# A hybrid attention and recurrence layer on one core: the same program, ordered by the scheduler's timeline mode

## The chip, the core and the metric

The kernel runs on one core of a Trainium2 chip. Its engines are TensorE (PE, with PEld for its weight loads), VectorE (DVE), ScalarE (ACT), GpSimd (POOL) and SyncE (SP), which issues all DMA transfers of this kernel from one queue. The metric is the device time of one execution in microseconds (us), as the median of several runs. A profile is one execution recorded by the hardware profiler; its times count from the first instruction.

## The reference

One layer over 16 learned meta tokens and 1024 frames of width 1024, all in float32, cut to what matters:

```python
u = rms_norm(h, norm_mix_w)
fq, fk, fv, ff, hq, hf, hi, hg = split(u @ w_in)
# A: forgetting attention, 8 heads x 64, causal; c = cumsum(log_sigmoid(ff + bias))
fox = softmax(fq @ fk.T / 8 + c_i - c_j, causal) @ fv
# B: gated recurrence, 4 heads with a 128 x 128 state
S_t = diag(f_t) S_{t-1} + k_t v_t^T;  o_t = S_t^T q_t
hgrn = rms_norm(o, hgrn_norm_w) * silu(hg)
h = h + concat(fox, hgrn) @ w_out
u = rms_norm(h, norm_ffn_w)
h = h + (silu(u @ w_gate) * (u @ w_up)) @ w_down      # inner width 2816
out = rms_norm(h, norm_final_w)[:, 16:]
```

## The kernel before

Every large matrix product is done in float32r in three passes: each operand is split into a high part (`hi`, a cast on ScalarE, L135) and the rest (`lo`, a subtraction on VectorE, L136), and `mm3` (L167 to L169) multiplies hi by hi, hi by lo and lo by hi into the same PSUM bank. So each tile that TensorE multiplies needs first a load, then ScalarE, then VectorE.

The program is written with a tile framework. The kernel's Python code records instructions stage by stage; the framework then gives each engine its own list, in an order that a scheduler chooses when the context is left, assigns the buffers of the pools, and adds the semaphore waits that the data and the buffers need. On the chip an engine works through its list strictly in that order: an instruction that waits holds up all that stand behind it on its engine, and a transfer that SP has not issued holds up all transfers behind it. The scheduler may move an instruction of a later stage ahead of an earlier one when it finds it ready. A few places are pinned by hand (`after`, `hold`, `keep_in_program_order`).

The stages, in the order in which the code records them:

- **Norm and first projection** (L219 to L256): RMSNorm of nine row tiles, transposes on TensorE, `hi` columns projected.
- **Recurrence** (`hgrn_proj` L349, `hgrn_compute` L398) of four heads, with `fox_v` (L310, the value projection of the attention, evacuated at L323 and L324) between them. A head's recurrence is a chain of small steps in two units of 512 frames: exponentials on ScalarE, adds on VectorE, small products on TensorE.
- **Attention** (`fox_compute` L627), four pairs of heads. `fox_proj` (L512) projects keys and queries of the next pair (bank `dense`, evacuated at L522/L523 and L530/L531). `fox_group` (L552) treats 256 queries of one head: scores on TensorE (L569, L570, bank `g`), added to the bias with a running minimum on VectorE (L575), exponential on ScalarE (L580), transposes back on TensorE (L588, L600, bank `tr`), split on ScalarE and VectorE (L604, L605; L590, L591), product with the values on TensorE (L610, bank `o`), sums on VectorE (L622, L639). The projection of a pair is independent of the attention of the pair before it, so it is work that TensorE can do while the attention waits for VectorE.
- **Output projection and second norm** (`out_proj` L735, `norm2` L761, `pair` L793), and the sums of the first blocks of the FFN.
- **FFN, gate and up** (L970, 22 blocks): products of half blocks by a scheme with seven instead of eight products; the weights' sums are made on VectorE (`ffn_sums`, L836 to L839), the results go to DRAM (`h_store`).
- **FFN, down** (L1149 on): 7 products of 6 pieces each. For each piece `stage` loads a part of the intermediate result (`h_st`, L992) and a part of `w_ffn_down`, splits both, and `mults` (L1024) multiplies: 24 matmuls for a full piece, 12 for the last of a product. The weight quarters B11, B12, B21, B22 are loaded ahead into buffers of their own (`fetch`, L984), six pieces each, and VectorE makes the combinations T1 to T4 of them (L1048, L1052, L1056, L1060), which later products use. A table (`work`, L1132) says at which piece the code records each load and combination: B12 at pieces 10 to 15, T1 at 15 to 20, and so on.
- **End**: the four row tiles of the last product are finished one after the other by hand (L1165 on), each with its sum, its norm (`final_half`, `final`) and its store.

## Time and profile before

| what | value |
|---|---|
| median of three runs | 1305.54 us (1304.8 to 1307.61) |
| the profiled execution, device time | 1305.52 us |
| its span, first to last instruction | 1303.8 us |
| busy: PE, DVE, ACT, POOL | 1270.7 (97%), 909.3 (70%), 621.2 (48%), 125.9 (10%) us |
| moved by DMA | 146.38 MB, 112 GB/s over the span |
| mean granted TensorE clock | 0.995 |

The profiled execution's 1305.52 us are its span and 1.7 us around it, and lie 0.02 us under the median. TensorE is busy nearly all of the span, so its list, and where that list has to wait, sets the time. The views used further on: the busy time of each engine in a stretch, groups of equal instructions with the mean time of one, and what ended the idle time before an instruction.

### The profile page before, as it was taken

What the parts mean: (1) busy time and instruction counts of PE and PEld (TensorE: products, weight loads), DVE (VectorE), ACT (ScalarE), POOL (GpSimd) and SP (SyncE); (2) the same over time, 40 slices, a digit from 0 to 9 for tenths busy, and PEclk for the clock granted to TensorE, in tenths of its full rate; (3) what the DMA queues carried; (4) which work ended last, traced back from release to release, by engine and by line L of the source; (5) the groups of instructions that cost most, each with busy time, mean ns of one, the idle gap of its engine ahead of it and who ended that gap; (6) DMA issues with size and microseconds to landing.
All of it is one profiled execution on the core that took longest, in us unless ns stands there. A gap on an engine that the chain in (4) does not pass through costs nothing.

```text
span 1303.8 us, 18528 instructions
## 1 busy us (share of the span) xinstructions
PE 1270.7 (97%) x6553; PEld 1065.4 (82%) x6553; DVE 909.3 (70%) x1889; ACT 621.2 (48%) x1334; POOL 125.9 (10%) x257
## 2 busy tenths in 40 slices
PE   7999999999999999899999999999999999999997
PEld 6888898988888888688868888888888888888886
DVE  6448657574687877796798766666666654697777
ACT  6347656464666665664453333233323323433364
POOL 1131101010334342210000000000000000000000
PEclk8999999999999999999999999999999999999999
DMA  7232212123321211633314323333332336954442
GB/s 253 73 98 58 74 44 73 58 58 118 92 79 45 69 52 47 187 100 119 125 49 138 125 83 115 121 111 103 118 121 74 113 121 248 317 188 151 121 169 82
DMA packets 135197, 146.38 MB, mean 112 GB/s; under 512 B 6984, under 2 KB 95368, under 8 KB 135104
## 3 DMA queue, kind: packets, MB, share of 16 engines
q1 hardware_dynamic: 135104, 145.19, 34.6%
q8 instruction: 52, 0.85, 0.3%
q14 instruction: 41, 0.34, 0.1%
HBM read 105.98 MB, written 39.19 MB: 111 GB/s over the span
## 4 chain that ended last, share of the span: by engine, by line
PE 80%; DVE 8%; ACT 5%; DMA 3%; issue 2%; POOL 2%; SPq 0%; POOLq 0%; DVEq 0%; ACTq 0%
PE pb L167 10%; PE pb L169 10%; PE pb L168 10%; PE dense L169 8%; PE dense L167 8%; PE dense L168 8%; PE g L169 4%; PE g L167 4%; PE g L168 4%; PE o L610 2%; PE tr L600 2%; PE g L569 1%; PE g L570 1%; PE g L446 1%; DMA w_st<-in_w_in_dram 1%
## 5 line engine op out<-in xcount | busy, mean ns | idle before, releaser
L167 PE MATMUL dense<-u_hi,w_hi 128*128 128x512 f32 (+2 forms) x384 | 141.7, 369 | 0.0
L169 PE MATMUL dense<-u_hi,w_lo 128*128 128x512 f32 (+2 forms) x384 | 141.3, 368 | 0.0
L168 PE MATMUL dense<-u_lo,w_hi 128*128 128x512 f32 (+2 forms) x384 | 140.9, 367 | 0.0
L168 PE MATMUL pb<-T_lo,bh 128*128 128x512 f32 x352 | 137.2, 390 | 0.2
L169 PE MATMUL pb<-T_hi,bl 128*128 128x512 f32 x352 | 137.1, 390 | 0.1
L167 PE MATMUL pb<-T_hi,bh 128*128 128x512 f32 x352 | 136.9, 390 | 0.2 <-ACT bh L135 0.2
L135 ACT CAST bh<-sS 128x512 fp32r<-128x512 f32 x88 | 54.3, 621 | 144.3 <-PE pb L168 70.3
L135 ACT CAST h_hi<-h_st 128x1024 fp32r<-128x1024 f32 (+1 forms) x43 | 41.8, 971 | 83.7 <-PE o L168 38.2
L168 PEld LDWEIGHTS pb<-T_lo,bh 128*128 128x128 f32 x352 | 66.1, 188 | 15.0 <-DVE T_lo L136 1.1
L169 PEld LDWEIGHTS dense<-u_hi,w_lo 128*128 128x128 f32 x384 | 72.9, 190 | 6.2
L167 PEld LDWEIGHTS pb<-T_hi,bh 128*128 128x128 f32 x352 | 66.1, 188 | 14.6 <-ACT bh L135 0.6
L167 PEld LDWEIGHTS dense<-u_hi,w_hi 128*128 128x128 f32 x384 | 72.6, 189 | 6.5
L168 PEld LDWEIGHTS dense<-u_lo,w_hi 128*128 128x128 f32 x384 | 72.6, 189 | 6.4
L169 PEld LDWEIGHTS pb<-T_hi,bl 128*128 128x128 f32 x352 | 66.1, 188 | 14.2 <-DVE bl L136 0.4
L167 PE MATMUL pb<-w_hi,h_hi 128*128 128x512 f32 x198 | 77.3, 391 | 0.0
L169 PE MATMUL pb<-w_hi,h_lo 128*128 128x512 f32 x198 | 77.2, 390 | 0.0
L168 PE MATMUL pb<-w_lo,h_hi 128*128 128x512 f32 x198 | 77.2, 390 | 0.0
L136 DVE TENSOR_TENSOR w_lo<-w_st,w_hi 128x1024 fp32r<-128x1024 f32 (+1 forms) x41 | 49.6, 1210 | 35.4 <-ACT w_hi L135 35.4
L136 DVE TENSOR_TENSOR h_lo<-h_st,h_hi 128x1024 fp32r<-128x1024 f32 (+1 forms) x43 | 48.3, 1124 | 30.2 <-ACT h_hi L135 29.9
L167 PE MATMUL g<-B_hi,w_hi 128*128 128x512 f32 x168 | 66.6, 396 | 0.9 <-ACT p L865 0.9
L169 PE MATMUL g<-B_hi,w_lo 128*128 128x512 f32 x168 | 66.5, 396 | 0.0
L168 PE MATMUL g<-B_lo,w_hi 128*128 128x512 f32 x168 | 66.3, 395 | 0.0
(861 smaller groups left out, 3328.5 us busy)
## 6 DMA issues: line engine op xcount, KB each, us to landing
w_st<-in_w_in_dram SPq DMA_DIRECT2D x24, 512.0 KB, 4.2
w_st<-in_w_ffn_gate_dram SPq DMA_DIRECT2D x22, 512.0 KB, 3.8
w_st<-in_w_ffn_up_dram SPq DMA_DIRECT2D x22, 512.0 KB, 3.9
B<-in_w_ffn_down_dram SPq DMA_DIRECT2D x20, 512.0 KB, 6.3
h_st<-S SPq DMA_DIRECT2D x20, 512.0 KB, 3.8
h_st<-A SPq DMA_DIRECT2D x15, 512.0 KB, 4.4
A<-g SPq DMA_DIRECT2D x22, 256.0 KB, 2.0
S<-u SPq DMA_DIRECT2D x22, 256.0 KB, 3.0
```

The costliest lines, as they stand in the source:

```text
L135: later(act.copy(hi, src))
L136: return later((engine or vec).tensor_sub(lo, src, f32(hi)))
L167: pe.matmul(o, lhsT=ah, rhs=bh, start=first, stop=False, skip_group_check=skip)
L168: pe.matmul(o, lhsT=ah, rhs=bl, start=False, stop=False, skip_group_check=skip)
L169: pe.matmul(o, lhsT=al, rhs=bh, start=False, stop=last, skip_group_check=skip)
L446: m = pe.matmul(gb[:, k * P:(k + 1) * P], lhsT=X[:, k * P:(k + 1) * P], rhs=X[:, 256 + k * P:256 + (k + 1) * P], start=True, stop=True)
L569: pe.matmul(sc[:, :w], lhsT=QA[:, P * i:P * (i + 1)], rhs=KS[:, c0:c0 + w], start=True, stop=False)
L570: pe.matmul(sc[:, :w], lhsT=QB[:, P * ii:P * (ii + 1)], rhs=KS[:, c0:c0 + w], start=False, stop=True)
L600: pe.transpose(pt[:, o + ii * P:o + (ii + 1) * P], Ss[ii][:, c:c + P], ident)
L610: m = pe.matmul(ob[:, q0:256], lhsT=vt[:, blk, :], rhs=r[:, q0:256], start=blk == NT, stop=blk == 2 * g + 1 and i == 3)
```

## The change

The context that records and orders the program is opened with another option. Nothing else is edited.

```diff
-    with _tile.TileContext(nc) as tc:
+    with _tile.TileContext(nc, schedule_with_timeline_sim=True) as tc:
         hybrid_trunk(tc, *args)
```

With the option the scheduler decides what is ready by a timeline of engines and transfers instead of a list of simple durations. The instructions are the same, 6329 matmuls, 1197 on ScalarE, 389 transfers and so on, with the same operands; their order on every engine differs, and with it which buffer each gets and when it comes free. The first 70 us and the gate-and-up stage keep nearly the same order. In the other stages the lists differ as these three places show.

**TensorE, attention of the third pair of heads.** `g_56..` and `g_57..` are score banks of that pair, `o_5626` its value product, `KS0_5233` its keys, and `dense_6103` the projection of the fourth pair. Before:

```order
L569 MATMUL g_5696<-KS0_5233,QA0_5235 128x392
L570 MATMUL g_5696<-KS0_5233,QB_5670 128x392
L167 MATMUL dense_6103<-u_hi_134,w_hi_6070 128x512
L610 MATMUL o_5626<-mz0_3670,v1_5316 128x256
L569 MATMUL g_5700<-KS0_5233,QA0_5235 128x392
L570 MATMUL g_5700<-KS0_5233,QB_5670 128x392
L168 MATMUL dense_6103<-u_lo_135,w_hi_6070 128x512
L610 MATMUL o_5626<-PH_5637,v1_5316 128x256
```

With the change the same scores and transposes stand without a projection between them:

```order
L569 MATMUL g_5700<-KS0_5233,QA0_5235 128x392
L570 MATMUL g_5700<-KS0_5233,QB_5670 128x392
L569 MATMUL g_5765<-KS1_5234,QA1_5236 128x328
L570 MATMUL g_5765<-KS1_5234,QB_5755 128x328
L600 MATMUL tr_5642<-ident_118,S__5601 128x128
L600 MATMUL tr_5642<-ident_118,S__5613 128x128 x2
L610 MATMUL o_5626<-mz0_3670,v1_5316 128x256
L569 MATMUL g_5769<-KS1_5234,QA1_5236 128x328
L570 MATMUL g_5769<-KS1_5234,QB_5755 128x328
```

The projection `dense_6103` now stands one pair earlier, in one run behind the transposes of the second pair (`S__4307`, `tr_4369`):

```order
L600 MATMUL tr_4369<-ident_118,S__4307 128x128
L600 MATMUL tr_4369<-ident_118,S__4323 128x128
L169 MATMUL dense_6074<-u_hi_134,w_lo_6065 128x348
L167 MATMUL dense_6103<-u_hi_134,w_hi_6070 128x512
L168 MATMUL dense_6103<-u_lo_135,w_hi_6070 128x512
L169 MATMUL dense_6103<-u_hi_134,w_lo_6071 128x512
```

So the projections, which were spread between the steps of the attention, are drawn together and earlier.

**VectorE, second product of the down stage.** `h_lo` and `w_lo` are the rests of the pieces that TensorE multiplies next; `T_k` and `B_k` (the tile's own number ends the name) are the combinations for later products. Before:

```order
L136 TENSOR_TENSOR h_lo<-h_st,h_hi 128x1024
L136 TENSOR_TENSOR w_lo<-B_3_11283,w_hi 128x1024
L1072 TENSOR_TENSOR r_11313<-r_11313,g 128x512
L136 TENSOR_TENSOR h_lo<-h_st,h_hi 128x1024 x2
L136 TENSOR_TENSOR w_lo<-B_4_11309,w_hi 128x1024
L136 TENSOR_TENSOR h_lo<-h_st,h_hi 128x512
L136 TENSOR_TENSOR w_lo<-B_5_11349,w_hi 128x512
L1048 TENSOR_TENSOR T_0_11646<-B_0_11467,B_0_11387 128x1024
```

With the change, from the same `w_lo` on:

```order
L136 TENSOR_TENSOR w_lo<-B_3_11283,w_hi 128x1024
L1060 TENSOR_TENSOR B_0_11165<-B_0_11387,B_0_11165 128x1024
L1048 TENSOR_TENSOR T_1_11685<-B_1_11505,B_1_11427 128x1024
L1048 TENSOR_TENSOR T_2_11721<-B_2_11531,B_2_11089 128x1024
L1052 TENSOR_TENSOR B_1_11427<-B_1_11429,T_1_11685 128x1024
L1056 TENSOR_TENSOR B_1_11505<-B_1_11429,B_1_11505 128x1024
L1052 TENSOR_TENSOR B_2_11089<-B_2_11469,T_2_11721 128x1024
L1056 TENSOR_TENSOR B_2_11531<-B_2_11469,B_2_11531 128x1024
L1048 TENSOR_TENSOR T_3_11746<-B_3_11570,B_3_11127 128x1024
L1060 TENSOR_TENSOR B_1_11205<-B_1_11427,B_1_11205 128x1024
L136 TENSOR_TENSOR h_lo<-h_st,h_hi 128x1024
```

Nine combinations now stand between that `w_lo` and the next `h_lo`, and five more (four of full size, one half) between it and the `h_lo` after it.

**SP, the same place.** `h_st<-A_0_68`, `A_1_69`, `A_2_70` are the loads of the first three pieces of the second product. Before:

```order
L992 DMA h_st<-A_0_68 128x2x512
L984 DMA B_2_11245<-in_w_ffn_down_dram 128x2x512
L1067 DMA r_11247<-h_dram 128x1024
L992 DMA h_st<-A_1_69 128x2x512
L984 DMA B_3_11283<-in_w_ffn_down_dram 128x2x512
L1067 DMA r_11285<-h_dram 128x1024
L992 DMA h_st<-A_2_70 128x2x512
```

With the change twelve weight loads stand between the first two of them, the last eleven of which are:

```order
L984 DMA B_0_11387<-in_w_ffn_down_dram 128x2x512
L984 DMA B_0_11389<-in_w_ffn_down_dram 128x2x512
L984 DMA B_1_11427<-in_w_ffn_down_dram 128x2x512
L984 DMA B_1_11429<-in_w_ffn_down_dram 128x2x512
L984 DMA B_0_11467<-in_w_ffn_down_dram 128x2x512
L984 DMA B_2_11469<-in_w_ffn_down_dram 128x2x512
L984 DMA B_1_11505<-in_w_ffn_down_dram 128x2x512
L984 DMA B_3_11507<-in_w_ffn_down_dram 128x2x512
L984 DMA B_2_11531<-in_w_ffn_down_dram 128x2x512
L984 DMA B_4_11533<-in_w_ffn_down_dram 128x2x512
L984 DMA B_3_11570<-in_w_ffn_down_dram 128x2x512
L992 DMA h_st<-A_1_69 128x2x512
```

The weights of four products are now asked for at the start of the second one.

## The prediction

> **What bounds the kernel now.** First the page's first lines, then the chain of waits that ended last.

> ```profile
> span 1303.8 us, 18528 instructions
> PE 1270.7 (97%) x6553; PEld 1065.4 (82%) x6553; DVE 909.3 (70%) x1889; ACT 621.2 (48%) x1334; POOL 125.9 (10%) x257
> PE 80%; DVE 8%; ACT 5%; DMA 3%; issue 2%; POOL 2%; SPq 0%; POOLq 0%; DVEq 0%; ACTq 0%
> ```

> TensorE is busy for 1270.7 of 1303.8 us. It idles 33.1 us, and that is all that an order can win; what it can lose is read from VectorE, the next busiest. Its 909.3 us would fit beside TensorE's work with room to spare, but only if they are spread well, so the second view is the windows by stage: microseconds, then each engine's busy time, the granted clock, the DMA share and GB/s.

> ```profile
> 0.00:100.00 100.00, 93.26 (x457) 77.49 (x458) 54.77 (x114) 48.20 (x98) 22.75 (x45) 0.97 0.45 143
> 100.00:357.00 257.00, 251.08 (x1604) 223.60 (x1603) 166.48 (x399) 152.98 (x469) 27.71 (x44) 1.00 0.23 69
> 357.00:592.00 235.00, 225.37 (x1413) 191.83 (x1413) 187.74 (x607) 149.89 (x335) 75.40 (x169) 1.00 0.28 85
> 592.00:700.00 108.00, 105.23 (x478) 83.65 (x477) 86.32 (x173) 51.44 (x113) 0.00 (x0) 1.00 0.31 99
> 700.00:1092.00 392.00, 391.82 (x1713) 321.09 (x1712) 260.02 (x385) 123.38 (x184) 0.00 (x0) 1.00 0.35 112
> 1092.00:1296.00 204.00, 203.94 (x896) 167.73 (x894) 150.40 (x202) 93.38 (x134) 0.00 (x0) 1.00 0.56 187
> 1296.00:1303.80 7.80, 0.00 (x0) 0.00 (x0) 3.59 (x14) 1.89 (x6) 0.00 (x0) 0.65 0.48 185
> ```

> Behind each window stand its length and TensorE's busy time. Their difference is TensorE's idle time: 6.7 us in the head, 5.9 in the recurrence, 9.6 in the attention, 2.8 in the output projection and the FFN's first blocks, 0.2 and 0.1 in the FFN's two halves, 7.8 behind the last matmul. VectorE (187.74 of 235, 86.32 of 108) is at 80% in the attention and from 592 to 700 us; there the lists must interleave well.

> What such interleaving does is seen in 50 us of the attention, first all instructions, then those on the projections' bank `dense` alone (no POOL column), and two shorter windows:

> ```profile
> 446.00:496.50 50.50, 49.76 (x322) 43.47 (x320) 38.14 (x134) 31.78 (x72) 20.14 (x42) 1.00 0.19 56
> 446.00:496.50 50.50, 27.88 (x112) 19.02 (x113) 5.17 (x9) 3.83 (x8) 1.00 0.19 56
> 526.00:530.00 4.00, 1.98 (x9) 1.38 (x10) 3.87 (x9) 3.31 (x7) 2.16 (x3) 1.00 0.90 220
> 659.00:685.00 26.00, 23.60 (x99) 17.15 (x98) 25.80 (x47) 16.65 (x31) 0.00 (x0) 1.00 0.16 41
> ```

> TensorE is full there because 112 projection matmuls fill it. Without them 22 to 26 us of it are left (27.9 us is an upper end, since overlapping spans of neighbours count; by starts they are 23.4) beside some 33 us of VectorE. The last two rows show what happens where VectorE has more than TensorE: VectorE at 97% and 99%, TensorE idle 2.0 and 2.4 us.

> **How the change is priced.** The instructions are the same, so none costs more or less; only waits come and go. For each TensorE instruction the new order and the waits tell the last VectorE (ScalarE) instruction that it needs, and for each of those the last TensorE instruction that must precede it. Between two such points both engines have a fixed set of instructions, each with its duration in this trace. Where VectorE has more than TensorE, TensorE idles at least for the difference; stretches that do not overlap add up. In the old order this count gives 5.3 us, at 526 to 530 us (2.4) and 659 to 685 us (1.7) nearly all, where the rows above show 2.0 and 2.4. In the new order it gives 76.0 us, 67.4 with VectorE alone. It is a lower bound: waits on transfers and hand-offs come on top.

> *Attention: 34.6 us.* The largest stretch is the one of the order shown above, the third pair without the fourth's projection. VectorE's part of it, by rows:

> ```profile
> L605 DVE TENSOR_TENSOR PL<-tr,PH 128x512 fp32r<-128x512 f32 (+1 forms) x80 | 49.1, 634 | 7.0 <-ACT PH L604 5.4
> L622 DVE TENSOR_TENSOR mixp<-mixp,o 64x256 f32<-64x256 f32 x32 | 13.3, 414 | 5.4 <-ACT mixp L621 4.8
> L591 DVE TENSOR_TENSOR mz<-tr,mz 16x256 fp32r<-16x256 f32 x32 | 13.2, 414 | 1.7 <-ACT mz L590 0.4
> L575 DVE CUSTOM_DVE_ANT_0 S__5958<-g,nl 128x456 f32<-128x456 f32 x1 | 0.6, 633 | 0.1
> L575 DVE DVE_READ_ACCUMULATOR2_ANT mx<- 128x1 f32 x41 | 3.4, 83 | 0.0
> ```

> 37 score steps L575 of 264 to 456 columns with their read-outs are 14.7 us, 16 L605 9.0 (both forms, the half-width ones shorter), 8 L622 3.2, 7 L591 2.9, and 13 small ones 4.1: 33.9 us. TensorE has 25.5 us of scores, transposes and value products: 8.4 us idle. In the other stretches of this stage VectorE stands against TensorE with 16.0 to 11.4, 13.4 to 9.6, 12.7 to 8.2, 7.6 to 6.1, 5.2 to 4.2 and 4.6 to 2.9 us, together 17.2; the remaining 9.0 us are short ones, half of them on ScalarE, some where the recurrence hands over. The projections, cover in the old order, are no saving where they now stand: they take the same time there, and L523 and L531 of each are still queued behind the scores' steps.

> *Recurrence: 11.7 us.* Where heads and their halves meet, TensorE's next projection waits for the value evacuation (L324) or for a gate step: 7.5 us of VectorE against 4.8, 2.6 against nothing, 7.6 against 5.9, and ScalarE with 2.6 against 0.4; the rest are smaller ones.

> *Output projection and FFN's first blocks: 11.8 us.* In 26 us VectorE now has the splits, sums and norms of the first blocks ahead of the first block product: 19.6 us against 11.1 in one stretch, 3.0 against 1.1 ahead of it.

> *Start of the down stage: 17.2 us.* VectorE's new list puts combinations ahead of the `h_lo` that the second product needs.

> ```profile
> L136 DVE TENSOR_TENSOR h_lo<-h_st,h_hi 128x1024 fp32r<-128x1024 f32 (+1 forms) x18 | 20.4, 1133 | 8.3 <-ACT h_hi L135 8.3
> L1048 DVE TENSOR_TENSOR T<-B,B 128x1024 f32<-128x1024 f32 (+1 forms) x6 | 6.8, 1133 | 1.2 <-DMA B<-in_w_ffn_down_dram 1.2
> L1052 DVE TENSOR_TENSOR B<-B,T 128x1024 f32<-128x1024 f32 (+1 forms) x6 | 6.6, 1132 | 0.0
> L1056 DVE TENSOR_TENSOR B<-B,B 128x1024 f32<-128x1024 f32 (+1 forms) x6 | 6.5, 1131 | 0.0
> L1060 DVE TENSOR_TENSOR B<-B,B 128x1024 f32<-128x1024 f32 x5 | 5.9, 1221 | 0.0
> 1092.00:1120.00 28.00, 28.00 (x125) 23.08 (x124) 15.78 (x17) 12.83 (x16) 0.00 (x0) 1.00 0.98 366
> ```

> From that `w_lo` to the second next `h_lo` stand 17 instructions: 14 combinations and three splits, one of them of half size, 19.0 us by these rows. TensorE has 32 matmuls meanwhile; the last row's 125 took 28.00 us, 0.224 us each, so 7.3 us: 11.7 idle. Three stretches just ahead of it add 2.5, 1.1 and 1.9 us. The combinations are then done and do not come back later, but TensorE was never short there before (0.1 us idle in 204), so no time returns.

> The transfers are a second route to the same wait: in SP's list 6.55 MB lie between the loads of the first and second piece, the second included. At the 366 GB/s of that row, where the queues were at 98%, they need 17.9 us, and TensorE has 24 matmuls, 5.4 us, of the first piece: a wait of 12.5 us. It lies beside the VectorE wait and is not added. If TensorE has nothing left when they start, it is up to the full 17.9 us, 5.4 more, which belongs to the upper end.

> *Gate and up: 0.* The order is nearly the same and the 0.2 us idle stays.

> *End: 2.5 us.* The four row tiles are finished in turns, with the last tile's steps behind those of the others.

> ```profile
> 1292.38 2.19 ACT L1115 ACTIVATE y<-y,rs_y 128x1024 f32<-128x1024 f32 x2 [0.49 <-DVE rs_y L110]
> 1298.00 0.20 ACT L105 ACTIVATE rs_y<-rs_v 128x1 f32<-128x1 f32 x1 [0.41 <-DVE rs_v L104]
> 1298.23 0.20 ACT L106 ACTIVATE rs_y<-rs_y 128x1 f32<-128x1 f32 x1
> 1299.32 0.72 ACT L1118 ACTIVATE y<-y,rs_y 128x512 f32<-128x512 f32 x1 [0.88 <-DVE rs_y L110]
> ```

> Before, the two multiplies L1115 (2.19 us) were done 3.4 us ahead of the last tile's L106. In the new list they stand in front of it: 2.2 us, and a few small steps on VectorE 0.3. Bounds: 0, if the waits left room for them, to 3.3.

> *The clock: 3.4 us.* The granted clock fell once in the head:

> ```profile
> 8.15:14.97 6.82, 4.57 (x15) 2.82 (x16) 5.83 (x12) 4.81 (x11) 1.34 (x2) 0.50 1.04 390
> PE g L569 <- DVE mx L575: 4.5, 8, 1.5
> PE dense L209 <- POOL um L249: 2.7, 1, 2.7
> PE tr L413 <- issue: 2.0, 1, 2.0
> ```

> For 6.82 us the clock was 0.50, with TensorE waiting 2.7 us in it; the later waits of up to 2.0 us, as the windows' 1.00 shows, lost nothing. A wait of 10 us at the down stage is longer than any of these, and I price one such fall at half of 6.82 us. [...]

> **The sum.** Idle in the head as before, 6.7; recurrence 5.9 + 11.7; attention 9.6 − 2.4 (the counted piece that the old order had there) + 34.6; 592 to 700 us 2.8 − 1.7 + 11.8; gate and up 0.2; down 0.1 + 17.2; end 7.8 + 2.5; clock 3.4: 110.2 us. With 1270.7 busy this is a span of 1380.9. The profiled execution took 1305.52 us, 1.7 over its span and 0.02 under the median, so the forecast is 1380.9 + 1.7 = 1383 us, 6% slower.

> The bounds: the old hand-offs kept in this sum (5.9 + 7.2 + 1.1 = 14.2) may vanish inside the new waits, and the clock may not fall: 1365. Upwards, VectorE does not fill its stretches. Three rows tell how full it is when close to the bound: the 99% above, and

> ```profile
> 500.00:580.00 80.00, 73.62 (x437) 60.67 (x435) 63.50 (x188) 50.03 (x108) 19.46 (x44) 1.00 0.39 119
> 429.90:446.50 16.60, 16.54 (x118) 14.54 (x116) 15.16 (x51) 11.55 (x23) 3.89 (x10) 1.00 0.23 69
> ```

> 79% and 91%. At 85 to 90% the some 150 us of VectorE in the counted stretches take 16 to 26 us more, less the hand-offs already in: 10 to 19 more, and three falls of the clock 10 us.

> **The rivals.**

> *Heavier, about 1405.* Each wait also delays what VectorE and ScalarE need from TensorE, so the stretches stretch. For it speaks the 79% row, against it the 97 to 99% rows, which are the ones in which TensorE really waited. 12 us of unfilled VectorE and three falls of the clock give 1383 + 12 + 10 = 1405.

> *Lighter, about 1350.* TensorE's side of each stretch is its start-to-start time in the trace with the waits taken out. If some of what I took for waits is TensorE's own work, part of the difference was never idle: take half of the attention's and the recurrence's count, 23 us, and the 14.2 less: 1346 to 1350. Against it: the two old pieces were as counted.

> *Faster, about 1287.* The mechanism is the drawn-together projections: keys and queries are ready early, the attention's score steps no longer wait for them, and TensorE's 18.3 us of idle from 100 to 700 us go: 1305.5 − 18.3 = 1287. It decides only if VectorE can do its 33.9 us in TensorE's 25.5, a quarter faster than its rows' fixed 634 and 414 ns; nothing in the trace does that.

> *No effect, 1305.* The new order would have to differ only where TensorE has slack. The lists shown differ where VectorE is at 80%, so this is nearly excluded.

> **How the numbers follow.** My forecast's case, 1383 with its own range of 1362 to 1399, gets 0.72; heavier (1400 and more) 0.17; lighter 0.06; faster 0.03; no effect 0.02. From 1362 to 1412 are left out about 0.11 below and 0.08 above. A measurement of this kernel tells about 0.2% from no change; faster by more than that is 0.03, within it 0.01 (half of the no-effect case), slower 0.96.

> **What the changed profile would show.** TensorE's busy time stays near 1271 us, and its idle time grows to about 110. In its waits L575, L605, L523 and L324 of VectorE lead, with some 42 us in the attention; around the second product of the down stage there are 15 to 20 us of idle, waiting for `h_lo` or `h_st`, and the clock dips there; gate and up stays full; the end behind the last matmul is about 10 us. I would be wrong if VectorE is under 85% in the attention's waits, if the down stage's wait is far from 17 (a late transfer would be the reason), or if TensorE's busy time itself moved.

## The result: 7.4% slower, and the profile after

| what | before | with the change |
|---|---|---|
| median | 1305.29 us | 1402.84 us |
| ratio, 95% interval | | 1.074, 1.0724 to 1.0756 |
| profiled execution: device time, span | 1305.52, 1303.8 | 1400.60, 1398.9 |
| TensorE busy, idle | 1270.7, 33.1 | 1293.4, 105.5 |
| mean granted clock | 0.995 | 0.973 |

The forecast was 1383 us, with 1362 to 1412 as its range. The result lies inside, but above the 1399 at which the prediction ended its own case, in the part that it gave the heavier rival with a chance of 0.17. Both medians are of four executions; one of the changed kernel took 1855.97 us at a mean granted clock of 0.649, and the ratio leaves it out. The page of the changed kernel begins:

```profile
span 1398.9 us, 18517 instructions
PE 1293.4 (92%) x6553; PEld 1084.1 (78%) x6553; DVE 906.8 (65%) x1889; ACT 619.3 (44%) x1334; POOL 125.4 (9%) x257
PE 77%; DVE 10%; DMA 7%; ACT 3%; issue 2%; SPq 0%; DVEq 0%; ACTq 0%
```

The span is 95.1 us longer. The same matmuls keep TensorE busy 22.7 us longer, and its idle time grows by 72.4. Two things have to be explained, then, not one; that TensorE's busy time itself moves was one of the prediction's signs of being wrong. The windows of the changed kernel, cut at landmarks (first recurrence transpose L413, first score L569, first output product, first block product `pb`, first and last matmul behind the FFN's first half):

```profile
0.00:111.53 111.53, 102.66 (x506) 84.67 (x506) 64.08 (x127) 56.93 (x117) 27.38 (x48) 0.97 0.44 135
111.53:368.81 257.28, 242.85 (x1554) 221.74 (x1553) 157.02 (x361) 139.35 (x427) 19.97 (x29) 0.99 0.21 63
368.81:553.78 184.97, 159.54 (x982) 135.77 (x980) 126.21 (x441) 103.56 (x246) 61.77 (x140) 0.96 0.20 62
553.78:742.18 188.40, 158.28 (x796) 126.51 (x794) 129.50 (x332) 93.64 (x210) 16.31 (x40) 0.95 0.31 97
742.18:1151.64 409.46, 409.46 (x1789) 335.94 (x1790) 271.18 (x409) 126.24 (x195) 0.00 (x0) 1.00 0.33 108
1151.64:1387.89 236.25, 220.64 (x936) 179.52 (x935) 154.72 (x201) 95.49 (x135) 0.00 (x0) 0.95 0.49 165
1387.89:1398.88 10.99, 0.00 (x1) 0.00 (x0) 4.10 (x22) 4.10 (x9) 0.00 (x0) 0.67 0.49 192
```

Length less busy time is TensorE's idle time: 8.9, 14.4, 25.4, 30.1, 0, 15.6 and 11.0 us. The kernel before has 8.7, 3.9, 6.8, 5.1, 0.7, 0 and 7.9 between the same landmarks. The column with the clock shows the second thing: 0.99, 0.96, 0.95 and 0.95 in the stages that wait, where before it was 1.00. What ended TensorE's waits:

```profile
PE pb L167 <- ACT h_hi L135: 13.7, 2, 9.0
PE g L569 <- DVE mx L575: 6.9, 19, 1.2
PE tr L600 <- DVE mz L591: 6.8, 11, 1.2
PE dense L167 <- DVE ht L757: 5.9, 2, 3.2
PE tr L787 <- DVE xn L778: 5.0, 1, 5.0
PE tr L507 <- ACT hE L504: 4.8, 2, 3.1
PE g L570 <- DVE QA L531: 4.6, 1, 4.6
```

Most are for VectorE, as forecast; the largest is for ScalarE's `h_hi` at the start of the down stage. Of the four lines that the prediction named, L575 leads; L605 ended 4.7 us of waits, L324 1.3 and L523 0.2.

In these stretches of the attention VectorE is nearly full while TensorE is not:

```profile
468.00:500.00 32.00, 26.06 (x163) 20.23 (x162) 28.67 (x105) 22.24 (x53) 11.84 (x29) 1.00 0.10 30
533.00:552.00 19.00, 15.53 (x101) 12.55 (x99) 16.36 (x58) 13.15 (x29) 6.59 (x16) 1.00 0.06 19
```

90% and 86% for VectorE, 81% and 82% for TensorE, in the stretches without projections. From 382 us to the first output product TensorE idles 17.7 us, and VectorE works during 91% of that time. In two other stretches it is not so:

```profile
366.00:381.00 15.00, 6.06 (x41) 4.79 (x40) 5.63 (x16) 7.11 (x28) 1.14 (x4) 0.78 0.06 20
654.00:677.00 23.00, 11.62 (x45) 8.82 (x44) 10.43 (x26) 9.39 (x23) 0.00 (x0) 0.78 0.22 69
```

Here the recurrence hands over to the attention, and the output projection meets the second norm. TensorE idles 8.9 and 11.4 us, with VectorE busy for only 38% and 45% of the time. What TensorE waits for are chains of short steps that go from engine to engine, not a full VectorE. In the second stretch two waits, 5.9 us together, are for VectorE's L757, which itself waits 6.5 us for the load of `ht`.

### The profile page after: what moved, and what is told of

Its sections match the earlier page's. It is cut to its first block, busy times and chain, and to the rows that moved or that the text cites. A ratio compares the mean times of both kernels' runs of the same rounds, so it can differ in the third digit from the quotient of the medians.

```text
span 1398.9 us, 18517 instructions
## 1 busy us (share of the span) xinstructions
PE 1293.4 (92%) x6553; PEld 1084.1 (78%) x6553; DVE 906.8 (65%) x1889; ACT 619.3 (44%) x1334; POOL 125.4 (9%) x257
## 3 DMA queue, kind: packets, MB, share of 16 engines
q1 hardware_dynamic: 135104, 145.19, 32.2%
## 4 chain that ended last, share of the span: by engine, by line
PE 77%; DVE 10%; DMA 7%; ACT 3%; issue 2%; SPq 0%; DVEq 0%; ACTq 0%
PE pb L169 10%; PE pb L167 10%; PE pb L168 10%; PE dense L167 9%; PE dense L169 9%; PE dense L168 8%; PE g L169 4%; PE g L168 4%; PE g L167 4%; PE o L610 2%; DMA B<-in_w_ffn_down_dram 2%; PE tr L600 1%; DVE PL L605 1%; DMA xt<-in_x_dram 1%; DMA w_st<-in_w_out_dram 1%
## 5 line engine op out<-in xcount | busy, mean ns | idle before, releaser
L135 ACT CAST bh<-sS 128x512 fp32r<-128x512 f32 x88 | 52.6, 618 | 98.5 <-DVE sS L837 78.4
L135 ACT CAST h_hi<-h_st 128x1024 fp32r<-128x1024 f32 (+1 forms) x43 | 41.8, 972 | 105.4 <-PE g L168 41.2
L167 PE MATMUL pb<-w_hi,h_hi 128*128 128x512 f32 x198 | 75.4, 400 | 13.7 <-ACT h_hi L135 13.7
L136 DVE TENSOR_TENSOR w_lo<-w_st,w_hi 128x1024 fp32r<-128x1024 f32 (+1 forms) x41 | 50.1, 1222 | 57.1 <-ACT w_hi L135 54.1
L135 ACT CAST w_hi<-w_st 128x1024 fp32r<-128x1024 f32 (+1 forms) x47 | 48.8, 1038 | 66.7 <-DMA w_st<-in_w_ffn_gate_dram 33.2
L136 DVE TENSOR_TENSOR h_lo<-h_st,h_hi 128x1024 fp32r<-128x1024 f32 (+1 forms) x43 | 48.2, 1121 | 46.2 <-ACT h_hi L135 46.1
## 6 DMA issues: line engine op xcount, KB each, us to landing
B<-in_w_ffn_down_dram SPq DMA_DIRECT2D x20, 512.0 KB, 10.1
```

The costliest lines, as they stand in the source:

```text
L135: later(act.copy(hi, src))
L136: return later((engine or vec).tensor_sub(lo, src, f32(hi)))
L167: pe.matmul(o, lhsT=ah, rhs=bh, start=first, stop=False, skip_group_check=skip)
```

## The clock

```profile
282.31:285.72 3.41, 1.10 (x4) 0.55 (x4) 2.22 (x4) 3.27 (x10) 1.08 (x1) 1.00 0.09 16
285.72:289.13 3.41, 2.94 (x14) 2.95 (x14) 2.83 (x6) 1.54 (x4) 0.00 (x0) 0.50 0.68 215
514.40:517.80 3.40, 1.84 (x13) 1.51 (x13) 3.34 (x6) 2.61 (x6) 0.71 (x2) 1.00 0.81 222
517.80:521.21 3.41, 3.21 (x24) 2.74 (x23) 2.27 (x13) 2.27 (x8) 1.41 (x5) 1.00 1.01 338
1183.43:1186.84 3.41, 1.14 (x6) 0.60 (x4) 3.41 (x5) 2.81 (x5) 0.00 (x0) 1.00 1.03 396
1186.84:1190.25 3.41, 0.99 (x2) 0.83 (x3) 1.86 (x3) 1.04 (x1) 0.00 (x0) 0.50 1.05 388
1197.07:1200.49 3.42, 0.00 (x0) 0.00 (x0) 3.42 (x4) 1.04 (x1) 0.00 (x0) 1.00 1.05 387
1200.49:1203.90 3.41, 0.00 (x0) 0.00 (x0) 3.41 (x4) 0.00 (x0) 0.00 (x0) 0.50 1.05 397
```

A window with 2.3 us idle (3.41 less 1.10) is followed by one at 0.50, one with 1.6 us idle is not. The changed kernel has nine such falls between the head and the last matmul, 18 windows or 61 us at half clock. Matmuls of 128x512 that follow each other without a wait start 427 ns apart in them, against 227 ns at full clock, so about half of TensorE's 40.2 us of busy time there is lost, an estimate of 20.1 us. With 0.5 more in the head that is 20.6 of the 22.7 us by which busy time grew.

## The experiments

In most runs all lists are held: after the program is recorded, each instruction gets an order-only link to the one ahead of it in a given list of its engine. Such a list can be the old order, the changed one, or one of them with the places of one stage refilled in the other's order. In two runs only TensorE's order is given, and the scheduler fits the other lists to it.

```diff
-        hybrid_trunk(tc, *args)
+        hybrid_trunk(tc, *args); _pin(tc, nc)
+def _pin(tc, nc):
...
+    for order in orders:
...
+        for x, y in zip(names, names[1:]):
+            tc.add_manual_dep(by[y], x, dep, reason="order")
```

**The option without its order** (timeline mode, all lists held to the old order).

> The timeline mode is on, and every engine's list is held to the old order by order-only links, so only the option is left of the change. If the change acts through the order alone: 1305 us, within 3 us of the kernel before. If the option also adds waits or other code: 1308 us or more.

1305.52 us, ratio 1.000 (0.9991 to 1.001). The option costs nothing but by the order.

**The changed kernel with the old down stage and end**, and **the kernel before with the new ones** (places of everything recorded behind the gate-and-up stage refilled).

> The changed kernel with all lists held, but the down stage and the end in the old order within their places. The changed kernel lost 15.6 us of idle, 7.0 us to the clock and 3.1 us at the end there. Theory (stages add up; a stage's loss sits in its own order): 1402.8 - 25.7 = 1377, and the earlier stages' idle and clock losses stay as they are. Rival (the loss is one of coupled lists, which comes back elsewhere): 1390 us or more.

> The kernel before with all lists held, but the down stage and the end in the changed order. Theory (stages add up): 1305.3 + 25.7 = 1331, with two waits of some 5 and 9 us at the start of the second product and a clock of 0.5 behind them. Rival (the earlier stages' changed order caused part of it): 1320 us or less.

1378.84 us, 24.0 less than the changed kernel, and 1325.84 us, 20.5 more than the kernel before (ratio 1.0161, 1.0146 to 1.0176). Undone or done alone, the stage is worth nearly the same: this stage's loss adds to that of the others to within 3.5 us. 1331 was 5 too high: the two waits came out at 11.0 us together instead of 13.7.

**SyncE's list alone**, at the down stage.

> The kernel before with all lists held, and only SyncE's list of the down stage in the changed order; VectorE, ScalarE and TensorE keep the old one. If the transfers queued ahead of the loads of the second product set the wait there: waits of some 4 and 9 us before that product's first pieces, released by h_st, and 1305.3 + 13 to 21 (clock included) = 1318 to 1326. If VectorE's combinations ahead of h_lo set it: the count of VectorE's work gives only 1.3 us here, so 1305 to 1308.

1323.57 us (1.0140, 1.0124 to 1.0155). With VectorE's combinations where they were, 18.2 of the 20.5 us are there. ScalarE's timeline of this run at the start of the second product:

```profile
1116.25 1.04 ACT L135 CAST h_hi<-h_st 128x1024 fp32r<-128x1024 f32 x1 [8.99 <-DMA h_st<-A]
1133.07 1.04 ACT L135 CAST h_hi<-h_st 128x1024 fp32r<-128x1024 f32 x1 [14.35 <-DMA h_st<-A]
```

Each cast waited for its load, and TensorE waited 3.2 and 9.3 us for the casts. In the changed kernel, by the timelines of ScalarE and VectorE, the combinations wait too, for loads of the same queue:

```profile
1204.97 1.04 ACT L135 CAST h_hi<-h_st 128x1024 fp32r<-128x1024 f32 x1 [6.82 <-DMA h_st<-A]
1195.61 1.23 DVE L1048 TENSOR_TENSOR T<-B,B 128x1024 f32<-128x1024 f32 x1 [5.15 <-DMA B<-in_w_ffn_down_dram]
1210.51 1.22 DVE L136 TENSOR_TENSOR h_lo<-h_st,h_hi 128x1024 fp32r<-128x1024 f32 x1
```

VectorE starts its row of combinations 5.15 us late and does `h_lo` 4.5 us behind `h_hi`; TensorE's wait for that `h_lo` is 1.9 us, against 13.7 for the two `h_hi`. The transfers are the wait; VectorE is second. Its new list was not run without SyncE's, so what the combinations would cost if the loads came in time is not shown.

The run also shows a second cause at the end. TensorE's last matmul ends at 1311.38 us, 10.3 before the end of the span, though ScalarE's last step L1118 starts 3.4 us behind it, as before. Three stores are issued together late, the last two behind them:

```profile
1314.10 1.64 SPq L1116 DMA_DIRECT2D out_dram<-y  x3
1315.79 1.17 SPq L1121 DMA_DIRECT2D out_dram<-y  x1
1317.01 1.18 SPq L1119 DMA_DIRECT2D out_dram<-y  x1
```

In the old list the first of the three is issued at 1293.56, ahead of the last matmul at 1295.94. So SyncE's order alone makes the end 2.5 us longer; in the changed kernel, with ScalarE's order too, it is 3.1.

**TensorE's attention order**, in the old mode.

> The kernel before in its old mode, with one link more: TensorE's instructions of the attention and the output weights keep the changed kernel's order among themselves; the scheduler fits the rest around them. Theory (the projections drawn together leave VectorE's work uncovered): the count of work between the waits rises from 5.3 to 35.8 us, 30.5 more; with two to six half-clock windows at 1.7 us, 3 to 10, that is 1339 to 1346. Rival (the loss needs the changed lists of the other engines too): 1320 or less.

1337.83 us (1.0248, 1.0233 to 1.0264), 32.8 us more and just under what was expected. Only TensorE's list was given, and the scheduler laid the others anew around it: in this trace 537 of VectorE's 1889 places and 305 of ScalarE's 1334 hold another step than before. So the run shows that the changed kernel's other lists are not needed for this loss. It does not show that moving matmuls does it with all else in place.

```profile
364.00:541.03 177.03, 151.44 (x951) 131.35 (x951) 122.95 (x427) 100.21 (x225) 58.77 (x130) 0.99 0.17 52
541.03:703.73 162.70, 150.16 (x796) 122.26 (x795) 123.09 (x319) 89.78 (x205) 17.77 (x40) 1.00 0.35 110
```

Idle are 25.6 and 12.5 us, 26 more than in the two stages before (6.8 and 5.1), where the count gave 30.5 more; of TensorE's waits in this run 15.3 us are for L575. While TensorE idles in these two windows, VectorE is busy 93% and 92% of the time, as it is when VectorE's work has no cover.

**Less work on VectorE**, in the changed order and in the old one.

```diff
-            last = vec.tensor_sub(lo[:, s0:], pt[:, s0:], f32(hi[:, s0:]))
+            last = vec.tensor_sub(lo[:, 384:], pt[:, 384:], f32(hi[:, 384:]))
...
```

Further lines of this edit make the value products read these 128 columns repeatedly, so the attention's low parts are left out.

> The changed kernel with all lists held; the split L605 on VectorE writes 128 columns of the low part instead of 256 to 512, and the value products read these repeated, so TensorE's work stays and the attention's low parts are left out. Each L605 falls from 634 to about 300 ns by the 1.0 ns a column of its two forms, 21 us in 80. Theory (VectorE's work is the longer side in stretches): the count falls from 76.0 to 68.3, and some clock windows are spared: 1402.8 - 8 to - 12 = 1391 to 1395. Rival (hand-offs between engines, not the amount of VectorE's work, make the idle time): 1400 or more.

> The same shortened L605 in the kernel before, with all lists held in the old order. Theory (VectorE's work is covered there, the count stays 5.3): 1305, within 2 us. Rival (hand-offs): a gain as large as in the changed kernel, whatever that is.

1394.40 us, 8.4 less than the changed kernel, as expected; but 1299.12 us in the old order (0.9955, 0.9939 to 0.9972), 5.9 less, which was not. The split had fallen from 634 to 290 ns, 27 us in 80:

```profile
L605 DVE TENSOR_TENSOR PL<-tr,PH 128x128 fp32r<-128x128 f32 x80 | 22.8, 290 | 14.1 <-ACT PH L604 12.3
```

In the old order TensorE's busy time in the attention fell by 4.5 us (181.0 to 176.5) and its idle time by 1.3, though its value products L610 took the same 280 ns. So there seem to be small holds inside what counts as busy, which the count of work does not see. The difference between the two gains, 2.5 us, is too small to say that the amount of VectorE's work, rather than the hand-offs, is what TensorE waits for. This pair is inconclusive; the run with TensorE's order, above, is the better evidence.

**The clock by itself**: stalls of known length in a full stage.

```diff
         p7 = bank2()
+        n_ = STALLS.get(m, 0)
+        if n_:
+            d1 = pe.matmul(p7[:, :P], lhsT=zero, rhs=zero, start=True, stop=True)
+            x_ = [pool.memset(zero, 0.0) for _ in range(3 * n_ - 1)]
+            d2 = pe.matmul(p7[:, :P], lhsT=zero, rhs=zero, start=True, stop=True)
...
         product(p7, S3, "T3")
```

`STALLS` gives 1 to 6, three times over.

> The kernel before with all lists held, and in 18 blocks of the gate-and-up stage, where TensorE idles 0.5 us in all, one wait is put in front of a product: a small matmul, 2, 5, 8, 11, 14 or 17 memsets of 0.205 us on GpSimd that wait for it, and a matmul that waits for them. Idle about 0.7, 1.4, 2.0, 2.6, 3.2 and 3.9 us, three of each, 41 us in all. Theory (the clock is set anew every 3.41 us by the idle time of the window before; from about 2 us it is half): no fall behind the 0.7 and 1.4, some behind 2.6, nearly all behind 3.9, about 7 falls at 1.7 us: 1305 + 41 + 12 = 1358. Rival (a whole window must be idle): a fall behind one or none of the 3.9, 1347.

1389.84 us (1.0648, 1.0632 to 1.0663), 32 more than expected. The six stalls of 0.6 and 1.4 to 1.7 us brought no fall; of the three of 2.2 us two did; all nine of 3.0, 3.8 and 4.6 us did. Windows of the grid of this run, a stall of 1.4, the 2.2 us stall without a fall, one of 3.0 and one of 4.6 us:

```profile
749.53:752.94 3.41, 1.98 (x11) 1.56 (x10) 1.54 (x3) 0.60 (x1) 1.02 (x5) 1.00 0.32 94
752.94:756.36 3.42, 3.42 (x16) 2.82 (x16) 1.29 (x2) 1.52 (x2) 0.00 (x0) 1.00 0.20 60
770.01:773.42 3.41, 1.68 (x9) 1.22 (x7) 2.29 (x4) 1.21 (x2) 1.26 (x7) 1.00 0.08 22
773.42:776.84 3.42, 2.94 (x14) 2.47 (x15) 0.00 (x0) 0.00 (x0) 0.37 (x2) 1.00 0.44 132
793.90:797.31 3.41, 0.46 (x3) 0.46 (x4) 0.62 (x2) 0.37 (x1) 2.25 (x11) 1.00 0.52 154
797.31:800.73 3.42, 3.42 (x10) 2.64 (x9) 0.00 (x0) 0.00 (x0) 0.00 (x0) 0.50 0.02 5
845.10:848.51 3.41, 0.00 (x0) 0.00 (x0) 0.49 (x1) 0.19 (x1) 2.66 (x14) 1.00 0.52 154
848.51:851.93 3.42, 2.48 (x7) 2.10 (x8) 0.00 (x0) 0.00 (x0) 0.71 (x4) 0.50 0.00 0
851.93:855.34 3.41, 3.41 (x10) 2.64 (x9) 0.00 (x0) 0.33 (x1) 0.00 (x0) 0.50 0.00 0
```

The 2.2 us stall without a fall was cut by the grid: 1.7 us in one window, 0.5 in the next. Where a stall reaches into the window that is already at half (the last three rows, 0.9 us idle in it), half clock lasts another window, so the 11 falls of the stage took 17 windows and by estimate 25 us, 2.3 us each instead of 1.7. The rest above the expectation: the stalls were 47 us, not 41; the 36 small matmuls took 11 us, which I had left out; and 3 us were lost to a fall in the attention. The four parts, 86 us, are the 84.8 by which the run is longer, to about 1 us: where nothing else limits, the lost clock is lost time.

**TensorE's old order**, under the timeline mode.

> The changed kernel with TensorE's whole list held to the old order; the timeline mode orders the other engines and the transfers around it. Theory (a wait comes from two lists that don't fit, so TensorE's old order alone doesn't bring the time back): the count is 50.3 us, 45 more than before, of it 20.8 in the down stage; with the end's 3 and a clock loss of 10 to 20 that is 1363 to 1373. Rival (TensorE's order is what costs): 1330 or less.

1384.84 us (1.0615, 1.0596 to 1.0634). The rival falls: putting TensorE's list right wins 18 of 97.5 us. The other lists are again the scheduler's (967 of VectorE's 1889 places differ from the kernel before), so the 18 us here and the 32.8 above are not shares of one loss. But the time is 12 to 22 us above what was expected. From the recurrence to the first blocks TensorE idles 53.0 us, 37 more than before, where the count rose by some 24 (45 less the 20.8 of the down stage); in the down stage it is 20.6 (20.8 counted). The longest waits of this run ahead of the down stage:

```profile
PE g L569 <- DVE mx L575: 11.7, 13, 5.1
PE pb L167 <- ACT T_hi L135: 5.1, 1, 5.1
PE o L494 <- DVE S L496: 4.6, 3, 3.9
```

Which of them the count misses I did not follow. It is a lower bound for the idle time, not for its rise: here the rise is 13 us above the count's, in the next run 7 below.

**The new head and recurrence alone.**

> The kernel before with all lists held, and the head and the recurrence in the changed order within their places. Theory: the count rises from 5.3 to 22.3 us, 17 more, and one to three half-clock windows cost 2 to 5: 1324 to 1327, with idle in the recurrence and the rest as before. Rival (only a delayed attention suffers): 1310 or less.

1322.09 us (1.0124, 1.0110 to 1.0138), 16.8 more and 2 under what was expected. The recurrence:

```profile
114.21:358.34 244.13, 229.53 (x1465) 208.79 (x1465) 151.89 (x356) 135.53 (x422) 16.65 (x28) 0.97 0.20 62
```

14.6 us idle, as in the changed kernel, and 0.97 clock. Over the whole run idle time grows by 10.0 us (33.1 to 43.1), where the count grew by 17, and busy time by 6.6 (1270.7 to 1277.3).

The runs with one stage in its new order lose 16.8 (recurrence), 32.8 (attention) and 20.5 us (down stage and end), 70 of 97.5. No run changes the output projection and the first blocks alone, so the other 27 us are not attributed.

**Filling the waits** with small matmuls, in the run with SyncE's new list and in the head of the kernel before.

```diff
+        new_ = [pe.matmul(pa[0][:, :P], lhsT=zero, rhs=zero, start=True, stop=True) for _ in range(FILL.get(j, 0))]
...
         mults(j)
```

> The kernel of the run with only SyncE's new list at the down stage (1323.6 us), with TensorE kept busy in its two waits of 3.2 and 9.3 us by 10 and 40 small matmuls of zeros into a bank that is free. The transfers come no earlier. Theory (the clock's fall is a loss of its own, behind the wait): the clock stays at 1.00 there and 3.5 us come back, 1319 to 1321. Rival (the lost clock is hidden by the same transfers, or the clock falls for another reason): 1323 or more.

> The kernel before with all lists held, and 12 small matmuls of zeros in front of the first L209, where TensorE waits 2.7 us in the head and then runs at half clock for 6.8 us (2.3 us lost). If the head is bound by TensorE behind that wait, the clock stays full and up to 2.3 us are won: 1303 to 1304. If later waits in the head (1.5 us at 25 us, for VectorE's u_lo) take it back: 1305, within 0.5.

1327.39 us, 3.8 more than without filling: a failed experiment. In the trace each of these matmuls is two records, and the line numbers are one higher:

```profile
1122.69 4.53 PE L1172 MATMUL pb<-zero 128*128 128x128 f32 x20 [6.17 <-DVE r L1073]
1132.53 9.10 PE L1172 MATMUL pb<-zero 128*128 128x128 f32 x80
```

The first filling had to wait itself, for the bank to be emptied by VectorE's L1073; that follows a copy on ScalarE, which stands behind the late cast. In this wait the clock still fell; the second took 9.1 us and ended 5 us behind the cast it was to bridge. The clock did stay at 1.00 in the second wait, but whether the lost clock of the down stage could be won back stays open.

In the head the clock stayed at 1.00 too, and the recurrence's first transpose came 1.1 us earlier, but the time was 1307.10 us, 0.16% more (1.0008 to 1.0025). No version here that does all of the work beats the kernel before.

## Why the forecast was right, and where its sum was off

| term of the sum, added to before | forecast | measured |
|---|---|---|
| recurrence, idle | 11.7 | 10.6 |
| attention, idle | 32.2 | 22.0 |
| output projection and first blocks, idle | 10.1 | 21.6 |
| head, gate and up, idle | 0 | −0.5 |
| down stage, idle | 17.2 | 15.6 |
| end | 2.5 | 3.1 |
| clock | 3.4 | 20.6 |
| other busy time | 0 | 2.1 |
| span | 77.1 | 95.1 |

- **The idle terms** came out at 72.4 us against 73.7, and that they fit so closely is luck. Divided behind the last value product L610, the changed kernel has the first two of these windows, the kernel before the other two:

```profile
368.81:647.00 278.19, 246.52 (x1472) 207.31 (x1471) 190.97 (x633) 154.19 (x354) 78.08 (x180) 0.98 0.25 77
647.00:742.18 95.18, 71.30 (x305) 54.97 (x303) 64.74 (x139) 43.02 (x102) 0.00 (x0) 0.91 0.28 88
341.05:584.20 243.15, 233.44 (x1468) 198.43 (x1467) 193.74 (x632) 154.50 (x354) 81.92 (x181) 1.00 0.28 84
584.20:671.45 87.25, 85.01 (x397) 68.22 (x397) 61.96 (x135) 42.33 (x101) 0.00 (x0) 1.00 0.37 117
```

  TensorE's idle time grows by 22.0 us in the attention, where 32.2 were forecast, and by 21.6 behind it, where 10.1 were: two misses of some 10 and 12 us that cancel. (The forecast divides these stages 8 us later, at 592 us of the kernel before.) Behind the attention, the stretch from 654 to 677 us alone idles 11.4 us in a chain of short steps and loads with VectorE at 45%; the count of work does not price such a chain.
- **The projections drawn together** are borne out as a mechanism: with TensorE's new order of the attention the kernel loses 32.8 us, and VectorE is busy 93% and 92% of the time in which TensorE idles there. What is not shown is how much of it the scheduler's new lists for the other engines add.
- **The down stage's** size was right and its cause was not. I counted VectorE's combinations and laid the transfers beside them. The run with SyncE's list alone shows that the transfers are the wait: 18.2 of 20.5 us, of it 12.5 in two waits, the size of the one wait that the prediction gave this second route, and 2.5 at the end. VectorE's list and the others add 2.3 on top of it. Two routes of similar length looked alike in the sum; only the order of one queue at a time told them apart.
- **The end** was priced by ScalarE's order. That order has a part: in the changed kernel ScalarE's L1118 starts 5.3 us behind the last matmul, before 3.4. But SyncE's order of the stores alone gives 2.5 of the 3.1 us.
- **The clock** is the step that failed in size: "one such fall" at 3.4 us, where nine came at 2.2 us each, 20.1 together. The price of one was too high (in the head, half of the 4.57 us of busy time is 2.3) and their number far too low. I concluded from waits of up to 2.0 us under full clock that waits of this size lose nothing. But the falls go with the idle time within one window of the grid, in one wait or in several: all 57 full-clock windows of the 14 profiles with 2 us idle or more were followed by half clock, in the changed kernel one with a single wait of 2.1 us and one with two of 1.3 and 1.0 us. No window has to be idle as a whole: two of the three stalls of 2.2 us, which fill no window of 3.41 us, were followed by half clock. The rival "heavier, about 1405" had three falls and the rest from VectorE; its time is near the result, its parts are not.

The lost clock is 20.6 us of TensorE's busy time by account. How much of it would come back as time if the waits stayed and only the clock held is not shown; the stalls show it for a stage that nothing else limits.

## What to carry to other kernels

Before an order is changed, count for each engine the work between the points where it waits for another: where VectorE's part is longer than TensorE's, independent matmuls must stand there, and a scheduler that draws them together removes the cover; TensorE's order of the attention alone cost 32.8 us here. Compare such a count with the result stage by stage, since a total can fit while its terms miss. Read the queue of the transfers as an engine of its own: with SyncE's list alone, where loads for later products stand ahead of the next one's, the kernel lost 18.2 of the 20.5 us of the down stage and the end. And price idle time on TensorE above its length when it reaches some 2 us within 3.4: by estimate 2.3 us more each time, in the stalls.

## What the runs showed of the hardware that I had not expected

Over the 14 profiles of this case the time from the first record of the clock up to the last matmul was cut into the windows of 3.413 us on which the clock changes. All 57 full-clock windows with 2 us idle or more were followed by half clock; with 1.75 to 2 us 14 of 19, with 1.5 to 1.75 us 8 of 25, below 1.5 one out of some 5200. A window at half clock with 0.66 us idle or more was followed by another, 56 times of 56; with less than 0.57, in all but one of 80 cases, by full clock. The grid lies differently in different executions (a change of clock lies 8.15 us behind the first instruction in the kernel before, 9.24 in the changed one), so the same wait can fall to half clock in one and not in the next: a pause in the attention, at 524 to 530 us in the kernel before, brought a fall in seven of the nine profiles with the old attention order, and none in those of the kernel before and of the option without its order. By half of TensorE's busy time in the slow windows, that is an estimate of 1.6 to 3.1 us of difference between executions of one order.
